# Taking the seven products of a gate-and-up block apart around the plain quarters, with two of its weight sums made by adding DMAs in place

## The chip, the cores and the metric

The kernel runs on one core of one Trainium2 chip. The metric is the device time of one execution in microseconds, lower is better.

## The reference

One layer of a streaming encoder on 256 tokens of width 2048, all in float32:

```python
x = x + 0.5 * swiglu(rms_norm(x, ffn1_norm), ffn1_w_gate, ffn1_w_up, ffn1_w_down)
...  # mixer: S5 state-space heads and stick-breaking attention heads, then w_out
x = x + 0.5 * swiglu(rms_norm(x, ffn2_norm), ffn2_w_gate, ffn2_w_up, ffn2_w_down)
...  # per-layer embedding
def swiglu(h, w_gate, w_up, w_down):
    return (jax.nn.silu(h @ w_gate) * (h @ w_up)) @ w_down
```

The hidden width of each FFN is 5632. The change lies in `h @ w_gate` and `h @ w_up` of both FFNs.

## The kernel before, in words

**Precision by splitting.** Each float32 operand is split into two parts, `hi` and `lo`, and a product is three matmuls: hi x hi, lo x hi, hi x lo. For a weight tile of 128x1024 (two rows of tiles of 512 columns) ScalarE casts `hi` (L181) and VectorE subtracts to get `lo` (L184); this pair of instructions is called a split below. The parts go to a ring of seven pairs of buffers, four named `whi`/`wlo` and three `shi`/`slo` (`weight_pair`), so splits can run ahead of the matmuls.

**Blocks.** `ffn` walks over 11 blocks of 512 hidden columns (`f`). A block multiplies the 256 tokens by a 2048x512 piece of the gate weights and one of the up weights. The depth of 2048 is cut into four quarters of 512 rows; one quarter of one weight is one load of 1 MB into a tile called `raw`, of which there are five. Loads are issued by SP.

**Plain quarters.** `column(side, kbs)` loads quarters `kbs` of gate (side 0) or up (side 1) and multiplies them directly: two halves, each one split and 12 matmuls.

**Groups of seven.** `chunk(kb)` takes quarter `kb` of gate and of up together as a 2x2 block matrix (b11 and b21 are the two halves of the gate quarter, b12 and b22 those of the up quarter) and uses a Strassen-Winograd form: seven products of six matmuls each in place of eight. The products are numbered 1 to 7 by the PSUM bank that they add up in. Four of them need sums of weights:

- product 5: t1 = b11 + b12
- product 6: t2 = t1 + b22
- product 4: t4 = t2 + b21
- product 7: b12 + b22

Before, the first three are made by VectorE in tiles called `sum` (L513), and the fourth by a DMA issued from POOL that adds b22 to b12 in place (L574). The products are traced in the order 1, 5, 6, 4, 2, 3, 7. The matching sums of the activations are made once per FFN (`sum_forms`).

**An ordinary block** is `chunk(0)`, gate quarters 2 and 3 plain, `chunk(1)`, up quarters 2 and 3 plain. Blocks `f` = 6 to 10 of the first FFN and 1 to 10 of the second are ordinary. In the first FFN, blocks 3 and 5 use one group (`single`), and the other early blocks none; in the second FFN block 0 has an order of its own with one `chunk`. The down projections use `chunk` too.

**The end of a block.** `opened` copies bank 1 and makes the running sums with banks 6 and 7, `gated` adds banks 2 and 4, applies Silu and takes bank 5, `ended` adds the double bank 3/8 (L683) and multiplies (L685), and `turned` transposes the result (L217). PSUM has four single banks (`acc`: 1, 2, 4, 5) and two double ones (`aux`: 6/7 and 3/8), all in use in a block.

**Order.** The framework plans the order of each engine's instructions and gives out buffer slots when the program is built; the trace order of the code is the priority. `step()` advances work that was put off (`put_off`) by one step; `tc.issue_after` holds an instruction behind another on its engine.

Of the kernel before, what the change touches and what calls it, by code (L numbers as in the profile page):

```python
# [13 lines left out]
ALU = mybir.AluOpType  # L14
# [19 lines left out]
def layer_kernel(ctx: ExitStack, tc: tile.TileContext, a: dict, shapes: dict, out: bass.AP):  # L34
    nc = tc.nc
# [34 lines left out]
    def com(tag):  # L70
        return get(comp, tag, *{"sg": (1024, 1), "h": (1024, 2), "sq": (NB, 1), "mid": (2048, 1)}[tag])

    def phase(name):
        return tc.tile_pool(name=name, bufs=1, reuse_waits="tile")
# [20 lines left out]
    def start(g):  # L95
        beside.append(g)
        return g

    def step():
        for g in list(beside):  # L100
            if next(g, beside) is beside:
                beside.remove(g)

    def finish(g):
        for _ in g:
            pass

    def put_off(steps, fn, *args):


        def g():
            for _ in range(steps):
                yield
            fn(*args)

        return start(g())
# [169 lines left out]
    ring = [None, 0]  # L286
# [25 lines left out]
    def weight_halves(w, k0, nk, n0, own=None):  # L312

        raw = wp.tile([P, 4, NB], F32, tag="raw", name=uid("raw"), bufs=5)
        nc.sync.dma_start(raw[:, :nk, :], quarter(w, k0 // 4, n0))
        return weight_split(raw, nk, own)

    def gemm_half(ps, half, ts, start, stop, cols=slice(0, NB)):

        (ahi, alo), (h, hi, lo) = half  # L320
        for j in range(2):
            for t in ts:
                lh = ahi[:, 2 * h + j, t * P : (t + 1) * P]
                ll = alo[:, 2 * h + j, t * P : (t + 1) * P]
                nc.tensor.matmul(ps[t], lhsT=lh, rhs=hi[:, j, cols], start=start and j == 0, stop=False)  # L325
                nc.tensor.matmul(ps[t], lhsT=ll, rhs=hi[:, j, cols], start=False, stop=False)  # L326
        for j in range(2):
            for t in ts:
                lh = ahi[:, 2 * h + j, t * P : (t + 1) * P]
                nc.tensor.matmul(ps[t], lhsT=lh, rhs=lo[:, j, cols], start=False, stop=stop and j == 1)  # L330
# [137 lines left out]
    class Seven:  # L468
# [97 lines left out]
        def chunk(self, kb, final=()):  # L566
# [21 lines left out]
                self.product(7, summed(2), b12, final)  # L588
            step()

        def column(self, side, kbs, final=False):

            zs = ((2, 4), (3, 8))[side]
            w, n0 = self.ws[side]
            for kb in kbs:
                part = self.act(kb)
                for half in list(weight_halves(w, 4 * kb, 4, n0)):
                    end = final and kb == kbs[-1] and half[0] == 1
                    for t in range(TT):
                        ps = self.bank(zs[t])  # L600
                        gemm_half({t: ps}, (part, half), (t,), self.begin(zs[t]), end)
                    step()

    shared = (1, 5, 6, 7)

    def ffn(i, xn, nxt, bg=None):
# [4 lines left out]
        alone = (3, 5) if bg else ()  # L611
# [21 lines left out]
        for f in range(NF):  # L633
            for kb, (at, steps) in enumerate(((2, 8), (5, 11))):
                if bg and f == at:
                    put_off(steps, lambda kb: sums.append(sum_forms(sevens, whole_rows(sevens, xn(kb), pinned=True), "h")), kb)
            if prep and f == early:
                finish(prep)
                side.close()
                prep = None  # L640
                turns = pools.enter_context(phase(f"turns{i}"))
                hp = pools.enter_context(phase(f"h{i}b"))
            if f >= early or f in alone:
                sg, hh = com("sg"), com("h")
                gate_cols, up_cols = ([u[:, t * NB : (t + 1) * NB] for t in range(TT)] for u in (sg, hh))

                def opened(s, g=gate_cols, u=up_cols):
                    nc.scalar.copy(g[0], s.bank(1))
                    nc.vector.tensor_tensor(out=u[0], in0=s.bank(6), in1=g[0], op=ALU.add)
                    nc.vector.tensor_tensor(out=u[1], in0=s.bank(7), in1=u[0], op=ALU.add)  # L650

                def gated(s, g=gate_cols, u=up_cols, hh=hh):
                    for z, (ps, other) in enumerate(((s.bank(2), g[0]), (s.bank(4), u[1]))):
                        nc.vector.tensor_tensor(out=g[z], in0=ps, in1=other, op=ALU.add)
                        nc.scalar.activation(g[z], g[z], AF.Silu, scale=xn.rs(z))
                    v = hh.rearrange("p (t n) -> p t n", t=TT)
                    nc.vector.tensor_tensor(
                        out=v, in0=s.bank(5).unsqueeze(1).to_broadcast([P, TT, NB]), in1=v, op=ALU.subtract
                    )

                s = Seven(xn, lambda kb: sums[kb], ((wg, f * NB), (wu, f * NB)), sevens, turns)
                if f == 0:
                    sums.append(sum_forms(sevens, whole_rows(sevens, xn(0))))
                    s.column(0, (1,))
                    s.column(1, (1,))
                    s.chunk(0, shared)
                    put_off(0, opened, s)
                    s.column(0, (2,))
                    s.column(1, (2,))
                    s.column(0, (3,), True)  # L670
                    sums.append(sum_forms(sevens, whole_rows(sevens, xn(1))))
                elif f in alone:
                    s.single(0, gate_cols[0], *up_cols)
                    s.column(0, (1, 2, 3), True)
                else:
                    s.chunk(0)
                    s.column(0, (2, 3))
                    s.chunk(1, (*shared, 2, 4))
                    put_off(0, opened, s)
                put_off(0, gated, s)  # L680

                def ended(s, g=gate_cols, u=up_cols, hh=hh, f=f, hp=hp):
                    nc.vector.tensor_tensor(out=hh, in0=s.banks[3.8], in1=hh, op=ALU.add)  # L683
                    for t in range(TT):
                        nc.vector.scalar_tensor_tensor(  # L685
                            out=u[t], in0=u[t], scalar=xn.rs(t), in1=g[t], op0=ALU.mult, op1=ALU.mult
                        )
                    put_off(2, turned, hp, f, hh)

                s.column(1, (1, 2, 3) if f in alone else (2, 3) if f else (3,), True)  # L690
                if f in alone:
                    put_off(0, ended, s)
                else:
                    ended(s)
                continue


            def gate():
                for t in range(TT):
                    nc.scalar.activation(sg[:, t * NB : (t + 1) * NB], pg[t], AF.Silu, scale=xn.rs(t))  # L700

            first = ()
            if f == 0:
                warm_up(10)
                first = first_quarters(wg, xn)
            pg = gemm_block(xn, wg, f * NB, KD, first)
            sg = com("sg")
            if f == 0:
                for n in range(ND):
                    put_off(n, load_x, n)  # L710
                    put_off(n + 2, xn.squares, n)
                put_off(6, gate)
            else:
                gate()
            pu = gemm_block(xn, wu, f * NB, KD)
            if prep and f == 0:
                start(prep)
            hh = com("h")
            for t in range(TT):
                nc.vector.scalar_tensor_tensor(  # L720
                    out=hh[:, t * NB : (t + 1) * NB], in0=pu[t], scalar=xn.rs(t),
                    in1=sg[:, t * NB : (t + 1) * NB], op0=ALU.mult, op1=ALU.mult,
                )
            put_off(2, turned, hp, f, hh)
# [42 lines left out]
        def summed(kb):  # L767
            if kb not in forms:
                forms[kb] = sum_forms(sevens, rows(kb))
            return forms.pop(kb) if kb == 0 or n else forms[kb]  # L770

        for n in range(0, ND, 2):
# [7 lines left out]
            s = Seven(kept, summed, ((wd, n * NB), (wd, (n + 1) * NB)), sevens, turns)  # L780
            plan = plans[n // 2]
            left = sum(kind == "s" for kind, _ in plan)
            for kind, kb in plan:
                final = (kind, kb) == plan[-1]
# [747 lines left out]
    for n, side in ((0, 0), (1, 0), (0, 1), (1, 1), (2, 0), (2, 1), (3, 0), (3, 1)):  # L1532
        y, r = ((yss, rss), (ysb, rsb))[side]
        ps = next(both) if n < 2 and not side else gemm_block(lambda k: y[k], sides[side], n * NB, SW // P)
        for t in range(TT):
            nc.vector.scalar_tensor_tensor(
                out=xt[t][n], in0=ps[t], scalar=r[0][:, t : t + 1], in1=xt[t][n], op0=ALU.mult, op1=ALU.add
# [73 lines left out]
    with sums_phase("sums3") as sevens:  # L1611
        forms = {1: sum_forms(sevens, whole_rows(sevens, npl(1)), "h")}
        s = Seven(npl, forms.get, ((wg, 0), (wg, NB)), sevens, sevens)
# [29 lines left out]
    s = small(1)  # L1643
# [21 lines left out]
    for c, (ahead, total) in enumerate(((early, part), (part, ms))):  # L1665
# [3 lines left out]
            out=com("sq")[:, :W], in0=gate[:, cols[c]], scalar=1.0, in1=gate[:, cols[c]], op0=ALU.mult, op1=ALU.mult,  # L1669
# [129 lines left out]
```

## Time and profile before

| | |
|---|---|
| median of 3 runs | 1819.23 us (1818.15 to 1820.26) |
| profiled execution | 1818.46 us |
| its span, first to last instruction | 1816.4 us |
| TensorE (PE) busy | 1806.7 us, 99% |
| VectorE (DVE) busy | 1573.9 us, 87% |
| ScalarE (ACT) busy | 1065.3 us, 59% |
| GpSimd (POOL) busy | 106.2 us, 6% |
| granted TensorE clock | 0.999 |

In rows of the profile an instruction is named by its line, engine, operation, and the tiles `out<-in`; `PEld` is the weight load of TensorE, which overlaps the matmuls. A row of instructions by group ends with the busy time, the mean of one in ns, and the idle time of the engine before them. Rows of a timeline begin with the start and the duration in us. A busy time of VectorE is the union of its instructions; the durations of two that follow each other overlap a little. "DMA to landing" is the time from the issue of a DMA to its completion.

The ordinary blocks of the first FFN lie at some 270 to 480 us of the span, those of the second at some 1070 to 1480 us.

### The profile page before, as it was taken

What the parts mean: (1) busy time and instruction counts of PE and PEld (TensorE: products, weight loads), DVE (VectorE), ACT (ScalarE), POOL (GpSimd) and SP (SyncE); (2) the same over time, 40 slices, a digit from 0 to 9 for tenths busy, and PEclk for the clock granted to TensorE, in tenths of its full rate; (3) what the DMA queues carried; (4) which work ended last, traced back from release to release, by engine and by line L of the source; (5) the groups of instructions that cost most, each with busy time, mean ns of one, the idle gap of its engine ahead of it and who ended that gap; (6) DMA issues with size and microseconds to landing.
All of it is one profiled execution on the core that took longest, in us unless ns stands there. A gap on an engine that the chain in (4) does not pass through costs nothing.

```text
span 1816.4 us, 24219 instructions
## 1 busy us (share of the span) xinstructions
PE 1806.7 (99%) x8918; PEld 1496.6 (82%) x8918; DVE 1573.9 (87%) x1839; ACT 1065.3 (59%) x1240; POOL 106.2 (6%) x162
## 2 busy tenths in 40 slices
PE   9999999999999999999999999999999999999998
PEld 7888888888888888888898888888888888888887
DVE  8978889999998896697567899999999999889775
ACT  7445455656565665455695566555565566567664
POOL 0020100000000001110021000000000010000000
PEclk9999999999999999999999999999999999999999
DMA  8799867777776667674636787787767787666563
GB/s 321 268 292 301 269 221 232 235 259 228 262 261 226 190 226 262 188 255 163 218 139 215 234 297 225 263 268 235 232 231 236 241 277 242 220 209 228 195 243 128
DMA packets 107655, 428.41 MB, mean 236 GB/s; under 512 B 24368, under 2 KB 48336, under 8 KB 65136
## 3 DMA queue, kind: packets, MB, share of 16 engines
q1 hardware_dynamic: 96256, 390.06, 60.8%
q0 software_dynamic: 10560, 35.40, 9.0%
q8 instruction: 70, 1.15, 0.2%
q10 hardware_dynamic: 720, 1.41, 0.2%
q14 instruction: 49, 0.40, 0.1%
HBM read 372.41 MB, written 10.88 MB: 211 GB/s over the span
## 4 chain that ended last, share of the span: by engine, by line
PE 96%; DVE 1%; DMA 1%; issue 1%; ACT 1%; SPq 0%; DVEq 0%; ACTq 0%
PE acc L325 16%; PE acc L326 16%; PE acc L330 16%; PE aux L330 7%; PE aux L326 7%; PE aux L325 7%; PE acc L509 5%; PE acc L506 5%; PE acc L507 5%; PE aux L509 3%; PE aux L506 3%; PE aux L507 3%; DMA raw<-in_ffn_w_gate 0%; PE aux L1210 0%; PE acc L1466 0%
## 5 line engine op out<-in xcount | busy, mean ns | idle before, releaser
L184 DVE TENSOR_TENSOR wlo<-raw,whi 128x1024 fp32r<-128x1024 f32 x480 | 580.7, 1222 | 123.5 <-ACT whi L181 120.5
L181 ACT CAST whi<-raw 128x1024 fp32r<-128x1024 f32 x480 | 498.2, 1050 | 291.9 <-PE acc L326 181.8
L325 PE MATMUL acc<-whi,nhi 128*128 128x512 f32 x908 | 356.3, 392 | 2.8 <-ACT whi L277 2.3
L326 PE MATMUL acc<-whi,nlo 128*128 128x512 f32 x908 | 353.7, 390 | 0.0
L330 PE MATMUL acc<-wlo,nhi 128*128 128x512 f32 x908 | 252.5, 389 | 0.0
L184 DVE TENSOR_TENSOR slo<-raw,shi 128x1024 fp32r<-128x1024 f32 x186 | 226.1, 1216 | 15.8 <-ACT shi L181 15.5
L181 ACT CAST shi<-raw 128x1024 fp32r<-128x1024 f32 x186 | 195.2, 1049 | 62.1 <-DMA raw<-in_ffn_w_down 20.3
L325 PEld LDWEIGHTS acc<-whi,nhi 128*128 128x128 f32 x908 | 170.4, 188 | 40.3 <-ACT whi L277 3.5
L330 PEld LDWEIGHTS acc<-wlo,nhi 128*128 128x128 f32 x908 | 170.3, 188 | 35.9 <-DVE wlo L184 0.3
L326 PEld LDWEIGHTS acc<-whi,nlo 128*128 128x128 f32 x908 | 170.5, 188 | 34.8 <-DVE nlo L278 0.3
L181 ACT CAST whi<-sum 128x1024 fp32r<-128x1024 f32 x79 | 83.3, 1054 | 159.6 <-DVE sum L513 141.5
L181 ACT CAST shi<-sum 128x1024 fp32r<-128x1024 f32 x59 | 62.1, 1053 | 104.0 <-DVE sum L513 90.8
L513 DVE TENSOR_TENSOR sum<-sum,raw 128x1024 f32<-128x1024 f32 x92 | 112.1, 1219 | 1.0
L184 DVE TENSOR_TENSOR wlo<-sum,whi 128x1024 fp32r<-128x1024 f32 x79 | 96.2, 1220 | 7.3 <-ACT whi L181 6.7
L574 POOL DMA_DIRECT2D raw<-raw x44 | 38.2, 867 | 1035.7 <-DVE sum L513 595.0
L325 PE MATMUL aux<-whi,nhi 128*128 128x512 f32 x220 | 85.6, 389 | 0.0
L326 PE MATMUL aux<-whi,nlo 128*128 128x512 f32 x220 | 85.6, 389 | 0.0
L184 DVE TENSOR_TENSOR slo<-sum,shi 128x1024 fp32r<-128x1024 f32 x59 | 72.0, 1220 | 1.2 <-ACT shi L181 0.5
L330 PE MATMUL aux<-wlo,nhi 128*128 128x512 f32 x220 | 67.7, 389 | 0.0
L325 PE MATMUL acc<-whi,hhi 128*128 128x512 f32 x156 | 60.7, 389 | 0.0
L326 PE MATMUL acc<-whi,hlo 128*128 128x512 f32 x156 | 60.7, 389 | 0.0
L513 DVE TENSOR_TENSOR sum<-raw,raw 128x1024 f32<-128x1024 f32 x46 | 56.0, 1217 | 5.1 <-DMA raw<-in_ffn_w_down 4.2
(390 smaller groups left out, 3404.1 us busy)
## 6 DMA issues: line engine op xcount, KB each, us to landing
raw<-in_ffn_w_up SPq DMA_DIRECT2D x88, 1024.0 KB, 5.8
raw<-in_ffn_w_down SPq DMA_DIRECT2D x88, 1024.0 KB, 4.9
raw<-in_ffn_w_gate SPq DMA_DIRECT2D x86, 1024.0 KB, 6.9
raw<-in_w_in SPq DMA_DIRECT2D x32, 1024.0 KB, 5.5
raw<-raw POOLq DMA_DIRECT2D x46, 512.0 KB, 5.6
raw<-in_w_out SPq DMA_DIRECT2D x16, 1024.0 KB, 4.9
raw<-in_w_ple_gate SPq DMA_DIRECT2D x16, 1024.0 KB, 5.5
hT<-mid SPq DMA_DIRECT2D x160, 64.0 KB, 4.8
```

The lines of the kernel that those rows point to most:

```text
L181: copy = nc.scalar.copy(hi, src)
L184: rest = nc.vector.tensor_tensor(out=lo, in0=src, in1=hi.bitcast(F32), op=ALU.subtract)
L325: nc.tensor.matmul(ps[t], lhsT=lh, rhs=hi[:, j, cols], start=start and j == 0, stop=False)
L326: nc.tensor.matmul(ps[t], lhsT=ll, rhs=hi[:, j, cols], start=False, stop=False)
L330: nc.tensor.matmul(ps[t], lhsT=lh, rhs=lo[:, j, cols], start=False, stop=stop and j == 1)
L506: nc.tensor.matmul(ps, lhsT=lh[j], rhs=hi[:, j], start=begin and j == 0, stop=False)
L507: nc.tensor.matmul(ps, lhsT=ll[j], rhs=hi[:, j], start=False, stop=False)
L509: nc.tensor.matmul(ps, lhsT=lh[j], rhs=lo[:, j], start=False, stop=z in final and j == 1)
L513: nc.vector.tensor_tensor(out=t, in0=x, in1=y, op=ALU.add)
L574: nc.gpsimd.dma_start(b12, b22, accum_op=ALU.add)
```

## The change

`front`, `middle` and `back` take the place of `chunk` in ordinary blocks; `chunk` stays for the other uses. The order of an ordinary block becomes: products 1, 2, 3 of group 0, gate quarter 2, products 5, 6, 4, gate quarter 3, product 7; then products 1, 2, 3 of group 1, up quarter 2, products 5, 6, 4, 7, up quarter 3. t1 is now made in place in b11 by a second adding DMA from POOL, issued ahead of the one for product 7; t2 and t4 are made by VectorE in place, in b11 and b21. The `sum` tiles are no longer used in these blocks. `opened` and `gated` come one plain quarter before the end of the block, not two.

```diff
+        def front(self, kb, final=()):
+
+            if ring[0] is None:
+                ring[:] = [self.turns, 0]
+            b11, b21, b12, b22 = self.load(kb)
+            whole, summed = self.lefts(kb)
+            self.product(1, whole(0, 0), b11, final)
+            nc.gpsimd.dma_start(b11, b12, accum_op=ALU.add)
+            nc.gpsimd.dma_start(b12, b22, accum_op=ALU.add)
+            step()
+            self.product(2, whole(1, 0), b21, final)
+            self.product(3, summed(3), b22, final)
+            step()
+            return (b11, b21, b12, b22), whole, summed, final
+
+        def middle(self, begun):
+
+            (b11, b21, b12, b22), whole, summed, final = begun
+            self.product(5, summed(0), b11, final)
+            nc.vector.tensor_tensor(out=b11, in0=b11, in1=b22, op=ALU.add)
+            self.product(6, summed(1), b11, final)
+            step()
+            nc.vector.tensor_tensor(out=b21, in0=b11, in1=b21, op=ALU.add)
+            self.product(4, whole(1, 1), b21, final)
+            step()
+
+        def back(self, begun):
+
+            (b11, b21, b12, b22), whole, summed, final = begun
+            self.product(7, summed(2), b12, final)
+            step()
...
-                    s.chunk(0)
-                    s.column(0, (2, 3))
-                    s.chunk(1, (*shared, 2, 4))
+                    begun = s.front(0)
+                    s.column(0, (2,))
+                    s.middle(begun)
+                    s.column(0, (3,))
+                    s.back(begun)
+                    begun = s.front(1, (*shared, 2, 4))
+                    s.column(1, (2,))
+                    s.middle(begun)
+                    s.back(begun)
                     put_off(0, opened, s)
                 put_off(0, gated, s)
...
-                s.column(1, (1, 2, 3) if f in alone else (2, 3) if f else (3,), True)
+                s.column(1, (1, 2, 3) if f in alone else (3,), True)
```

## The prediction

> **What bounds the kernel now.** I read the head of the page first, then busy time by stretches, then the waits of the matmul queue in the two stages that the change touches.
>
> ```profile
> span 1816.4 us, 24219 instructions
> PE 1806.7 (99%) x8918; PEld 1496.6 (82%) x8918; DVE 1573.9 (87%) x1839; ACT 1065.3 (59%) x1240; POOL 106.2 (6%) x162
> PEclk9999999999999999999999999999999999999999
> ```
> ```profile
> 150.00:1700.00 1550.00, 1549.17 (x7756) 1285.68 (x7751) 1361.35 (x1432) 916.53 (x1041) 90.61 (x126) 1.00 0.70 234
> ...
> 1170.14:1251.74 81.60, 81.60 (x362) 67.57 (x360) 78.97 (x77) 47.72 (x51) 3.47 (x4) 1.00 0.74 242
> 1251.74:1333.34 81.60, 81.60 (x362) 67.57 (x360) 79.12 (x77) 48.14 (x51) 3.49 (x4) 1.00 0.76 248
> 1333.34:1414.94 81.60, 81.60 (x362) 67.57 (x360) 78.78 (x77) 46.34 (x50) 3.48 (x4) 1.00 0.74 242
> sum 244.80, PE 244.80 PEld 202.70 DVE 236.87 ACT 142.21 POOL 10.43; mean PE 81.60 PEld 67.57 DVE 78.96 ACT 47.40 POOL 3.48
> ```
> ```profile
> PE acc L509 <- DVE slo L184: 0.4, 1, 0.4
> ```
>
> In the second fence the columns are the stretch, its length, then busy time of PE, weight loads, DVE, ACT and POOL, the granted clock, the DMA share and GB/s. From 150 to 1700 us the matmul queue is idle for 1550.00 - 1549.17 = 0.83 us in all, at a full clock. The three lower stretches are each two gate-and-up blocks of the second FFN: 40.80 us a block, no idle matmul time. A block has 14 products of six matmuls and four plain quarters of 24, so 180 matmuls, and 40.80 / 180 = 0.2267 us each. The last fence is the only wait of the matmul queue between 1040 and 1500 us. So TensorE sets the time, and the edit leaves its 180 matmuls a block as they are. The whole gain within reach is under 0.83 us. What I have to find out is whether the new order still feeds TensorE in time.
>
> By the Trainium skill, page "Trainium Kernel Development and Optimization", section Performance Expectations, busy matmul time is a bad measure of nearness to the limit, and the share of the weight loads a good one. By that rule the 82% of the weight loads would leave room for a gain; but every block here has the same 40.80 us for the same 180 matmuls, and the edit shortens none, so the rule earns only the small chance for "faster" below.
>
> The next engine is VectorE (DVE): 236.87 / 6 = 39.5 us of each 40.8, so 1.3 us are free per block.
>
> **What a block costs on VectorE.** Its instructions in the first of those stretches (two blocks), and their pace when nothing stands between them:
>
> ```profile
> L184 DVE TENSOR_TENSOR wlo<-raw,whi 128x1024 fp32r<-128x1024 f32 x18 | 21.5, 1215 | 0.1
> ...
> L513 DVE TENSOR_TENSOR sum<-sum,raw 128x1024 f32<-128x1024 f32 x8 | 9.7, 1217 | 0.0
> ...
> L513 DVE TENSOR_TENSOR sum<-raw,raw 128x1024 f32<-128x1024 f32 x4 | 4.9, 1216 | 0.0
> L685 DVE SCALAR_TENSOR_TENSOR h<-h,sm,sg 128x512 f32<-128x512 f32 x4 | 2.8, 743 | 0.0
> L217 DVE STREAM_TRANSPOSE mid<-h 128x512 f32<-128x512 f32 x4 | 2.6, 684 | 0.0
> L683 DVE TENSOR_TENSOR h<-aux,h 128x1024 f32<-128x1024 f32 x2 | 2.4, 1220 | 0.1
> ```
> ```profile
> 1161.98 1.22 DVE L184 TENSOR_TENSOR wlo<-raw,whi 128x1024 fp32r<-128x1024 f32 x1
> 1163.12 1.22 DVE L184 TENSOR_TENSOR slo<-raw,shi 128x1024 fp32r<-128x1024 f32 x1
> 1164.26 1.21 DVE L184 TENSOR_TENSOR wlo<-raw,whi 128x1024 fp32r<-128x1024 f32 x1
> ```
>
> A subtraction or a sum of 128x1024 lasts 1.22 us but follows the one before at 1.14 us, so I cost each at 1.14. Each block has 12 / 2 = 6 sums.
>
> **Part 1: one sum of three leaves VectorE in each group.** The edit touches the ordinary blocks: 5 of the first FFN (f = 6 to 10) and 10 of the second (f = 1 to 10), 15 blocks, 30 groups. Two sums a block go: 2 x 1.14 = 2.3 us. The two that stay write in place; their shape is that of the L513 rows, so I cost them as those. VectorE then needs 39.5 - 2.3 = 37.2 us, and 3.6 us of 40.8 are free. By itself this is worth nothing to the time, since no matmul waits for a sum now.
>
> **Part 2: one adding DMA more in each group, in series.** Now b11 += b12 must land before product 5 can be split, and b12 += b22 cannot start before that, since it overwrites what the first reads. The rows are those of the one adding DMA that a group has now, in the second FFN's blocks (1160 to 1480 us), then in the first's (280 to 440 us):
>
> ```profile
> L574 POOL DMA_DIRECT2D raw<-raw x15: 857/867/882, 1167.2 to 1451.7; - x15
> ...
> DMA to landing us min/median/max: 4.5/6.6/7.6
> ...
> L574 POOL DMA_DIRECT2D raw<-raw x8: 847/856/881, 287.6 to 426.9; - x8
> ...
> DMA to landing us min/median/max: 4.5/7.1/9.0
> ```
> ```profile
> q0 software_dynamic: 10560, 35.40, 9.0%
> ```
> ```profile
> raw<-in_ffn_w_up SPq DMA_DIRECT2D x88, 1024.0 KB, 5.8
> ...
> raw<-in_ffn_w_gate SPq DMA_DIRECT2D x86, 1024.0 KB, 6.9
> ```
> ```profile
> L181 ACT CAST whi<-raw 128x1024 fp32r<-128x1024 f32 x480 | 498.2, 1050 | 291.9 <-PE acc L326 181.8 <-PE aux L326 37.0 <-DMA raw<-in_ffn_w_down 17.5
> ```
>
> Call L the time from issue to landing: 6.6 us in ten blocks, 7.1 in five. I take these medians, not the ends 4.5 and 9.0, since they are of the same transfer in the same place; the ends go into the range. POOL's 0.87 us of issue lies inside L, and POOL has 94% of its time free. In the queue behind the second DMA, which waits on POOL for the first, stands only the next group's first.
>
> What the transfers add to the load: 9.0% of 1816.4 us for 35.40 MB is 4.6 us of all 16 engines per MB, 2.4 us for 0.524 MB; two more a block are 4.8 of 40.8 us, so the DMA share goes from about 0.75 to 0.87. It does not fill up, but it speaks for L as now or longer, not shorter.
>
> Now the wait. After product 1's split, VectorE has four splits before product 5's: products 2 and 3 and the two halves of the plain quarter, 4 x 1.14 = 4.6 us. Product 5's cast (1.05 us) starts when the DMA lands, L after product 1's split. So VectorE stands idle for L + 1.05 - 4.6. In the first group of a block the tail of the block before fills this: the aux sum, two multiplications and two transposes, (2.4 + 2.8 + 2.6) / 2 = 3.9 us. In the second group nothing does: opened and gated need products 6 and 7, which come later. Idle time there: 3.1 us at L = 6.6, 3.6 us at 7.1.
>
> Then the second DMA. After the landing VectorE has product 5's split, two sums and the splits of 6 and 4: 1.05 + 5 x 1.14 = 6.75 us. Product 7's split needs the second landing, L after the first, plus the cast: a further idle L + 1.05 - 6.75. In the first group a plain quarter's two splits (2.3 us) lie between and fill it; in the second group product 7 follows product 4 at once. Idle time: 0.9 us at 6.6, 1.4 us at 7.1.
>
> Together VectorE needs 37.2 + 4.0 = 41.2 us a block in the second FFN and 37.2 + 5.0 = 42.2 in the first, against 40.8 of TensorE: late by 0.4 and 1.4 us. **Sum of part 2:** 10 x 0.4 + 5 x 1.4 = 11 us. It comes to nothing where 2L + 2.1 - 4.6 - 6.75 stays under the free 3.6, so for L up to 6.4 us, and the order may let splits of the last quarter go ahead. At the largest landing of the second FFN, 7.6 us, it is 2.4 us in each of 15 blocks, 36 us; at 9.0 us it is 5.2 us, 78 us.
>
> By the Trainium skill, page "DMA: Bandwidth & Descriptors", section "Anatomy of one DMA — SWDGE (gpsimd) path", such a transfer takes about 2.0 us and its bytes at 436 GB/s, which would be 3.2 us for 0.524 MB, and the sum would be 0. The rows disagree: no landing is under 4.5 us.
>
> **Part 3: what is moved.** Products 2 and 3 with their casts and subtractions come ahead of 5, 6 and 4, and the quarters go between. SP issues its eight weight loads a block in the same order as now. But an up tile is held until product 7, a whole quarter longer, and there are five tiles. If the load for the up column's first new quarter has to take that tile, it is issued at product 7's split, while TensorE has products 7, 1, 2 and 3 before it, 4 x 1.36 = 5.4 us; it needs 5.8 + 1.05 us, so the splits must be 1.4 us ahead. How far ahead they are now, at worst (VectorE's subtraction, then the matmul that reads it):
>
> ```profile
> 1241.35 1.18 DVE L184 TENSOR_TENSOR wlo<-raw,whi 128x1024 fp32r<-128x1024 f32 x1
> ```
> ```profile
> 1243.12 0.39 PE L509 MATMUL aux<-wlo,nhi 128*128 128x512 f32 x1
> ...
> 1234.06 0.39 PE L506 MATMUL acc<-shi,hhi 128*128 128x512 f32 x1
> ```
> ```profile
> 1234.26 1.23 DVE L683 TENSOR_TENSOR h<-aux,h 128x1024 f32<-128x1024 f32 x1
> ```
>
> That is 1243.12 - 1242.53 = 0.6 us, at the seventh product of a dense group. In the new order two quarter splits (2.3 us) stand before product 7 against 5.4 us of matmuls, so 3.1 us are gained just there, and I cost the loads at nothing. With that cover gone and a load of 6.9 us, the lack is 2.5 us a block, 38 us.
>
> Product 3 opens the double bank as third product now, 2.7 us into a block, not sixth. The bank is free when the aux sum (begun 0.20 us into the block, 1.23 us long) is done at 1.4 us. One 1.14 us instruction ahead of it fits; a second would make it 1.0 us late, 15 us over 15 blocks. If the other double bank is taken, freed a quarter earlier, nothing. I take nothing.
>
> **The sum.** Span 1816.4, and 2.1 us around it in the profiled execution (1818.46), plus 11 gives 1829.5; the median of the three runs, 1819.23, is 0.8 above that execution: 1830.3 us.
>
> **The rivals.**
> - No change (0.38): the landings stay hidden, because they come under 6.4 us (4.5 is seen) or the last quarter's splits fill the gap. For it: TensorE now runs through blocks in which VectorE has only 1.3 us free, and gets 2.3 more. Against: medians 6.6 and 7.1, and more DMA load. Time 1819.2. This is the side other than my forecast's; it decides at L = 6.4. The 3.2 us of the Trainium skill's page on DMA would lead here too.
> - The tile ring (0.13): the up quarter's load waits for product 7's split and lands late, 38 us: 1857. For it: loads of 5.8 to 6.9 us against 5.4 us. Against: 3.1 us gained just before.
> - The double bank (0.06): 15 us, 1834.
> - Faster (0.03): at most the 0.83 us, so it needs something that no row shows.
>
> **How the numbers follow.** The forecast, VectorE starved by the two landings in a row, has 0.40 and its own range from 1820 to 1855 (L of 6.4 to 7.6). A change under 0.2% (3.6 us) cannot be told from none here. Slower: 0.40 + 0.13 + 0.06 = 0.59; within: 0.38; faster: 0.03. The range goes from the unchanged time, 1817.5, to 1860, past the tile ring; beyond lie the 78 us of 9.0 us landings and the faster case, under 2 in 10 together.
>
> **What would show it.** Of part 1: two sums fewer a block, VectorE busy for 37.2 us of it. Of part 2: 30 more adding DMAs; the casts of products 5 and 7 waiting for raw<-raw, most in the second group; the matmul queue waiting for casts and subtractions by some 0.4 to 1.4 us a block, which makes blocks of 41.2 to 42.2 us. Landings under 6.4 us, or blocks of 40.8 us, prove the forecast wrong. Waits of the matmul queue behind loads of in_ffn_w_up would show the tile ring; behind L683, the double bank.

## The result, and the profile after

The changed kernel takes 1944.47 us (1944.03 to 1946.56, four runs), the kernel before 1819.10 in the same rounds: a ratio of 1.0691, 95% interval 1.0673 to 1.0710. The change costs 125 us, where 11 were forecast. The head of the page, and busy time by stretches with the columns as in the prediction:

```profile
span 1942.3 us, 24188 instructions
PE 1856.1 (96%) x8918; PEld 1508.9 (78%) x8918; DVE 1543.1 (79%) x1809; ACT 1061.5 (55%) x1240; POOL 131.8 (7%) x192
PEclk9999999999999999999999999999898999999999
```
```profile
150.00:1700.00 1550.00, 1471.58 (x7232) 1192.22 (x7215) 1220.36 (x1288) 836.50 (x952) 113.61 (x153) 0.98 0.71 226
265.00:560.00 295.00, 270.38 (x1128) 214.66 (x1127) 233.52 (x226) 147.79 (x156) 22.40 (x29) 0.97 0.76 231
560.00:1090.00 530.00, 529.92 (x3056) 443.13 (x3055) 411.01 (x478) 327.41 (x410) 39.35 (x53) 1.00 0.63 214
1090.00:1620.00 530.00, 476.28 (x1954) 373.75 (x1953) 406.20 (x400) 255.29 (x272) 38.95 (x48) 0.96 0.74 226
```

The span grew by 1942.3 - 1816.4 = 125.9 us. PE idle grew from 9.7 to 86.2 us, by 76.5. The other 49.4 us stand in the same 8918 matmuls: PE is busy for 1856.1 in place of 1806.7. The granted clock tells of much of it: 1.00 in the stretch between the two FFNs, 0.97 and 0.96 where the ordinary blocks are. In the trace's clock records the clock is at half in 12 stretches of 3.41 or 6.83 us, 61.4 us in all, and PE is busy for 53.7 us of them at half the pace, so about 27 us are lost to it; before there is none in these stages. Where the other 22 us of longer busy time come from was not followed up. VectorE, which the forecast made the bound, is less busy than before.

What the matmul queue waits for, and below it what the casts and subtractions wait for (in total us, times, longest):

```profile
PE acc L506 <- ACT shi L181: 18.7, 8, 4.5
PE acc L506 <- ACT whi L181: 18.6, 8, 4.0
PE aux L506 <- ACT whi L181: 14.8, 9, 3.0
PE aux L506 <- ACT shi L181: 6.2, 7, 1.3
PE acc L325 <- DVE sg L686: 5.7, 2, 3.3
PE acc L506 <- DVE sg L686: 5.4, 6, 1.4
```
```profile
DVE wlo L184 <- ACT whi L181: 232.1, 128, 8.1
...
ACT whi L181 <- DMA raw<-raw: 127.4, 22, 9.0
...
ACT shi L181 <- DMA raw<-raw: 67.7, 16, 8.0
...
ACT whi L181 <- DVE raw L610: 33.9, 12, 5.0
```

The chain is read from below: the casts wait for the adding DMAs (`raw<-raw`) and for the in-place sum that makes product 6's weights (L610), VectorE waits for the casts, and so does the first matmul of a product (L506). The row of the first adding DMA (L598, b11 += b12), by its source line:

```profile
L598 POOL DMA_DIRECT2D raw<-raw x30: 852/858/882, 266.6 to 1574.7; - x30
...
who waited for it (us, times):
  POOL raw L599: 148.8, 17
  ACT whi L181: 93.5, 16
  ACT shi L181: 54.0, 11
...
DMA to landing us min/median/max: 4.6/9.4/11.5
```

Its median is 9.4 us, longer than any landing quoted before the change; the second (L599) has 4.5/5.5/12.2. Adding up, in the 14 ordinary blocks whose order of products could be followed in the trace, what each matmul started later than 0.2267 us after the one before it gives 113 us: in group 0 39.4 at product 4, 15.4 at product 6, 11.3 in the plain quarter behind product 4, 6.8 at product 2; in group 1 23.6 at product 4, 12.5 at product 6, 2.8 at product 7. Product 5, for which the first DMA works, costs nearly nothing: the plain quarter ahead of it still feeds PE.

**One block in detail.** SP's loads and POOL's adding DMAs, then ScalarE, VectorE and PE (start, duration, and in brackets the idle time before with its releaser), in group 0 of a block of the second FFN:

```profile
1340.20 1.46 SPq L315 DMA_DIRECT2D raw<-in_ffn_w_gate  x2
1343.61 0.33 SPq L520 DMA_DIRECT2D raw<-in_ffn_w_gate  x1
```
```profile
1345.12 0.86 POOL L598 DMA_DIRECT2D raw<-raw  x1 [11.04 <-DVE wlo L184]
1356.06 0.89 POOL L599 DMA_DIRECT2D raw<-raw  x1 [10.08 <-DMA raw<-raw]
```
```profile
1355.76 1.05 ACT L181 CAST whi<-raw 128x1024 fp32r<-128x1024 f32 x1 [8.72 <-DMA raw<-raw]
```
```profile
1356.85 1.23 DVE L184 TENSOR_TENSOR wlo<-raw,whi 128x1024 fp32r<-128x1024 f32 x1 [5.20 <-ACT whi L181]
1357.99 1.22 DVE L689 TENSOR_TENSOR h<-acc,h 128x1024 f32<-128x1024 f32 x1
1359.12 1.22 DVE L610 TENSOR_TENSOR raw<-raw,raw 128x1024 f32<-128x1024 f32 x1
1360.26 1.22 DVE L721 TENSOR_TENSOR h<-aux,h 128x1024 f32<-128x1024 f32 x1
1361.53 1.22 DVE L184 TENSOR_TENSOR slo<-raw,shi 128x1024 fp32r<-128x1024 f32 x1
1362.67 1.41 DVE L723 SCALAR_TENSOR_TENSOR h<-h,sm,sg 128x512 f32<-128x512 f32 x2
1364.00 1.30 DVE L217 STREAM_TRANSPOSE mid<-h 128x512 f32<-128x512 f32 x2
1365.22 1.18 DVE L613 TENSOR_TENSOR raw<-raw 128x1024 f32<-128x1024 f32 x1
```
```profile
1367.53 0.80 PE L506 MATMUL acc<-whi,hhi 128*128 128x512 f32 x1 [3.99 <-ACT whi L181]
```

The DMA is issued at 1345.12, when product 1's subtraction has read b11; three loads of 1 MB were issued in the 5 us before. It lands after 10.6 us. Then everything is a chain: product 5's cast and subtraction, the in-place sum for product 6, its split, the in-place sum for product 4 (L613). Between them stand pieces of the end of the block before (L689, L721, L723, L217). VectorE is busy without a gap from 1356.85 on, and still product 4 comes 4 us late. By stretches just behind that:

```profile
1360.00:1367.40 7.40, 2.94 (x11) 1.48 (x9) 7.35 (x9) 2.96 (x4) 0.00 (x0) 0.87 0.07 15
1367.40:1370.80 3.40, 3.27 (x8) 2.60 (x9) 3.40 (x4) 3.40 (x5) 0.00 (x0) 0.50 0.60 120
...
1374.20:1377.60 3.40, 3.40 (x17) 2.82 (x16) 1.67 (x3) 2.00 (x2) 0.00 (x0) 1.00 1.10 218
```

After the gap the clock is 0.50 for a whole stretch: 8 matmuls in 3.4 us where the row with the full clock has 17. The Trainium skill, page "TensorE: Matmul & The Clock Gate", section "Part 1: The HAM clock gate", has the clock at half after an idle window of about 3.4 us and until some 3.4 us of work. The trace agrees on half and on steps of 3.41 us; single gaps of 2.24 to 3.00 us brought it too, so one gap need not be 3.4 us long.

In group 1 the order on the engines adds to it. POOL, then the casts, then VectorE:

```profile
1278.55 0.87 POOL L599 DMA_DIRECT2D raw<-raw  x1 [5.79 <-issue]
```
```profile
1290.42 1.04 ACT L181 CAST whi<-raw 128x1024 fp32r<-128x1024 f32 x1 [7.69 <-DMA raw<-raw]
```
```profile
1281.62 1.23 DVE L613 TENSOR_TENSOR raw<-raw 128x1024 f32<-128x1024 f32 x1
1282.76 1.23 DVE L184 TENSOR_TENSOR wlo<-raw,whi 128x1024 fp32r<-128x1024 f32 x1
1291.49 1.23 DVE L184 TENSOR_TENSOR wlo<-raw,whi 128x1024 fp32r<-128x1024 f32 x1 [7.51 <-ACT whi L181]
```

Product 4's sum (L613) is ready at 1282.85, but its cast does not follow: in the order that the planner made, product 7's split stands ahead of product 4's. Its cast waits for the second landing and starts at 1290.42, 11.9 us after that DMA's issue and 7.6 us after product 4's sum was ready.

### The profile page after: what moved, and what is told of

Its sections match the earlier page's. It is cut to its first block, busy times and chain, and to the rows that moved or that the text cites. A ratio compares the mean times of both kernels' runs of the same rounds, so it can differ in the third digit from the quotient of the medians.

```text
span 1942.3 us, 24188 instructions
## 1 busy us (share of the span) xinstructions
PE 1856.1 (96%) x8918; PEld 1508.9 (78%) x8918; DVE 1543.1 (79%) x1809; ACT 1061.5 (55%) x1240; POOL 131.8 (7%) x192
## 3 DMA queue, kind: packets, MB, share of 16 engines
q0 software_dynamic: 14880, 51.13, 12.5%
## 5 line engine op out<-in xcount | busy, mean ns | idle before, releaser
L184 DVE TENSOR_TENSOR wlo<-raw,whi 128x1024 fp32r<-128x1024 f32 x531 | 642.3, 1225 | 231.8 <-ACT whi L181 229.0
L181 ACT CAST whi<-raw 128x1024 fp32r<-128x1024 f32 x531 | 549.0, 1049 | 504.3 <-PE acc L326 177.6
L181 ACT CAST shi<-raw 128x1024 fp32r<-128x1024 f32 x225 | 233.6, 1048 | 187.4 <-DMA raw<-raw 67.7
L184 DVE TENSOR_TENSOR slo<-raw,shi 128x1024 fp32r<-128x1024 f32 x225 | 273.2, 1220 | 74.1 <-ACT shi L181 68.5
L330 PEld LDWEIGHTS acc<-wlo,nhi 128*128 128x128 f32 x912 | 172.1, 189 | 36.2
L506 PE MATMUL acc<-whi,hhi 128*128 128x512 f32 x140 | 56.7, 405 | 14.0 <-ACT whi L181 10.3
L325 PE MATMUL acc<-whi,hhi 128*128 128x512 f32 x156 | 60.8, 390 | 2.4 <-DVE sg L686 2.4
L326 PE MATMUL acc<-whi,hlo 128*128 128x512 f32 x156 | 60.7, 389 | 0.0
L325 PE MATMUL aux<-whi,hhi 128*128 128x512 f32 x152 | 59.1, 389 | 0.0
L326 PE MATMUL aux<-whi,hlo 128*128 128x512 f32 x152 | 59.1, 389 | 0.0
L184 DVE TENSOR_TENSOR hlo<-hT,hhi 128x1024 fp32r<-128x1024 f32 x44 | 53.7, 1221 | 3.9 <-ACT hhi L181 3.9
L598 POOL DMA_DIRECT2D raw<-raw x30 | 25.9, 862 | 449.1 <-DVE wlo L184 242.1
L506 PE MATMUL acc<-shi,hhi 128*128 128x512 f32 x92 | 38.3, 416 | 18.4 <-ACT shi L181 17.5
L507 PE MATMUL acc<-whi,hlo 128*128 128x512 f32 x140 | 55.7, 398 | 0.0
```

Source lines behind the costliest of these rows:

```text
L181: copy = nc.scalar.copy(hi, src)
L184: rest = nc.vector.tensor_tensor(out=lo, in0=src, in1=hi.bitcast(F32), op=ALU.subtract)
L506: nc.tensor.matmul(ps, lhsT=lh[j], rhs=hi[:, j], start=begin and j == 0, stop=False)
L507: nc.tensor.matmul(ps, lhsT=ll[j], rhs=hi[:, j], start=False, stop=False)
L598: nc.gpsimd.dma_start(b11, b12, accum_op=ALU.add)
```

## The experiments

All are timed against the kernel before in common rounds. The texts on record use letters: A is the late landing of the first adding DMA, the others stand for the theory that the same text describes.

**The order alone.** The new order of the products and quarters, with the sums as before (three by VectorE in tiles of their own, one adding DMA):

```diff
-            nc.gpsimd.dma_start(b11, b12, accum_op=ALU.add)
+            t1 = self.add(b11, b12)
             nc.gpsimd.dma_start(b12, b22, accum_op=ALU.add)
...
-            nc.vector.tensor_tensor(out=b11, in0=b11, in1=b22, op=ALU.add)
+            t2 = self.add(b11, b22)
...
-            nc.vector.tensor_tensor(out=b21, in0=b11, in1=b21, op=ALU.add)
+            t4 = self.add(t2, b21)
```


> The new order alone: products 1, 2, 3, plain quarter, 5, 6, 4 and so on, but the sums as before (three by VectorE in sum tiles, one adding DMA for product 7). Theory A (the first adding DMA lands too late, behind weight loads that were issued at the same moment, and products 6 and 4 wait for the sums made from it): no such DMA is left, so 1817 to 1826 us. Rival B (the order itself costs: up tiles held longer, PSUM banks freed later, the block's tail in front of the sums): still above 1890 us. Rival C (two landings in a row starve VectorE before product 7, the prediction's term): 1817 to 1826 us, like A.

1818.86 us, ratio 1.0004 (0.9994 to 1.0013). The order costs nothing and earns nothing; the double bank and the tile ring of the prediction's rivals are no matter of the order.

**Each adding DMA by itself.** First the first one replaced by a sum in place on VectorE, then the second:

```diff
-            nc.gpsimd.dma_start(b11, b12, accum_op=ALU.add)
+            nc.vector.tensor_tensor(out=b11, in0=b11, in1=b12, op=ALU.add)
             nc.gpsimd.dma_start(b12, b22, accum_op=ALU.add)
```


> The changed kernel with only its first adding DMA (b11 += b12) replaced by a sum of VectorE in place; order, in-place sums and the second adding DMA stay, VectorE makes three sums as before. Theory A (the first landing comes too late for products 6 and 4): 1817 to 1826 us, no wait of the matmul queue at products 6 and 4. Rival D (writing the sums in place is itself a cost, since the raw tiles are then held until product 4): above 1840 us.

1831.43 us, ratio 1.0066 (1.0051 to 1.0081). Of the 125 us, 113 go with the first adding DMA. It is 12.6 us above the run of the order alone, which differs from it only in that t1, t2 and t4 have tiles of their own: that is what the sums in place cost, more than A had said and less than D. In place, a sum must wait until the split of the product before has read the tile; the casts wait 86.2 us, in 25 waits, for the sum of product 6 (L610). They also wait longer for loads of `in_ffn_w_up` (41.6 us against 14.9 with the order alone). Which of the two makes the 12.6 us was not separated.

```diff
-            nc.gpsimd.dma_start(b12, b22, accum_op=ALU.add)
...
+            nc.vector.tensor_tensor(out=b12, in0=b12, in1=b22, op=ALU.add)
             self.product(7, summed(2), b12, final)
```


> The changed kernel with its second adding DMA replaced by a sum of VectorE in place just before product 7; the first stays. A: the first DMA still lands late, perhaps a little sooner with less traffic, so most of the loss stays, 1890 to 1945 us. B: no change, 1935 to 1950. C: the second landing was the cause, so 1820 to 1840 us.

1915.02 us, ratio 1.0528 (1.0513 to 1.0544): the second DMA carries 29 us beside the first. Without the first it costs nothing that shows, since the run of the order alone has it too; so the 113 and the 29 us do not add up. The first lands as late as in the changed kernel, by its source line:

```profile
DMA to landing us min/median/max: 4.5/9.4/11.8
```

**Fewer loads beside it.** The plain quarters read one kept tile:

```diff
+                        keep[0] = wp.tile([P, 4, NB], F32, tag="raw", name=uid("raw"), bufs=5)
+                        nc.sync.dma_start(keep[0], quarter(wg, 2, f * NB))
...
-                    s.column(0, (2,))
+                    s.column(0, (2,), kept=keep[0])
```


> The changed kernel with the plain quarters of ordinary blocks multiplied from one weight tile that is loaded once per FFN, so four of eight weight loads a block are left out (four raw tiles are left for the rest) and the result is another. A: with fewer loads queued beside it the first adding DMA lands in 4.5 to 6.5 us instead of 9.4, and the time falls to 1820 to 1850 us. B: the order is the same, so it stays above 1900. C: both landings get shorter, 1820 to 1850.

1866.16 us, ratio 1.0263 (1.0247 to 1.0278). The row of the first adding DMA:

```profile
DMA to landing us min/median/max: 4.5/5.9/9.2
```

The adding DMAs and sums are the same, and 78 of 125 us are gone: most of the loss hangs on the loads beside the DMA, and the landing's median falls with them. They change something else too: the casts wait 4.7 us for loads of `in_ffn_w_up`, 36.2 in the changed kernel. How much of the 78 us that makes was not separated. But 47 us stay, so with a median of 5.9 us, under the 6.4 us at which the prediction had put the loss at nothing, the kernel is still well behind.

**The same DMA, earlier.** One adding DMA, b12 += b11, issued about a plain quarter and a product earlier, when the group's tiles have been loaded and before product 1; product 7's sum goes to a tile of its own:

```diff
+        def ready(self, kb):
...
+            b11, b21, b12, b22 = self.load(kb)
+            seven = self.add(b12, b22)
+            nc.gpsimd.dma_start(b12, b11, accum_op=ALU.add)
...
                     s.middle(begun)
+                    s.ready(1)
                     s.column(0, (3,))
```


> One adding DMA per group as in the second run (b12 += b11 here, for product 5), but the tiles are loaded and this DMA is issued about one plain quarter and a product ahead of the group, since it no longer waits for product 1's split; VectorE makes product 7's sum into a sum tile and the other two in place, so three sums. A: the landing is as late after its issue as ever, 6 to 10 us, but in time for products 6 and 4, so 1817 to 1835 us, against 1915 with the same count of DMAs and sums issued after product 1. If the adding DMA as such is the cost (contention with the weight loads, rival G): 1890 us or more.

1840.98 us, ratio 1.0117 (1.0102 to 1.0132), against 1915.02 with the same numbers of adding DMAs and sums: 74 us are back, so an adding DMA is not dear in itself. Not all of the 74 belong to the earlier issue: this run also takes product 7's sum out from behind the landing, and holding that sum back earns 32 us alone in a run below. A's range is missed by 6 us. The landing is 5.5 us in the median, up to 11.0; of the 22 us above the kernel before, PE's waits explain about 16 (21.1 us in all their rows, against 4.8 before), the largest of them for casts; which sum makes those late was not settled.

**More matmuls ahead of the sums.** In group 0 both gate quarters come before products 5, 6 and 4:

```diff
-                    s.column(0, (2,))
+                    s.column(0, (2, 3))
                     s.middle(begun)
-                    s.column(0, (3,))
                     s.back(begun)
```


> The changed kernel with both gate quarters of group 0 ahead of products 5, 6 and 4, so that the first DMA of group 0 has two plain quarters (10.9 us of matmuls) of cover instead of one; group 1 is untouched. A: the waits at products 6 and 4 of group 0 go (with the slow matmuls behind them some 66 of the 113 us counted in 14 blocks), 1865 to 1885 us. B: tiles are held still longer and the loads come later, 1945 us or more. C: product 7 now follows product 4 at once in both groups, so the second landing shows twice, 1950 to 1980 us.

1889.54 us, ratio 1.0391 (1.0374 to 1.0408): 55 us better than the change, and above A's range by 5 us. Products 6 and 4 of group 0, late by 54.8 us in the changed kernel, are late by under 2 us here, as A had it; group 1 still has 24.7 us at product 4, and its product 7 becomes later (11.3 us). Waits for the bank (`PE acc L506 <- DVE sg L686`) grew from 5.4 to 9.4 us.

**Product 7 held behind product 4, and the tail put off.**

```diff
+            copied, rest = self.last
+            with tc.issue_after(copied), tc.issue_after(rest):
-            self.product(7, summed(2), b12, final)
+                self.product(7, summed(2), b12, final)
```


> The changed kernel with product 7's cast and subtraction held behind product 4's on their engines (in group 1 the planned order has them ahead of product 4's, so product 4 stands behind the wait for the second landing). If that order carries the second landing's part of the loss (E, order of product 7 and 4): group 1's waits go, 36 of 113 us counted there, so 1905 to 1920 us, the same as the run in which VectorE made that sum. If it is the landing as such (C), holding product 7 back only moves the wait to product 7: 1935 us or more.

1931.77 us, ratio 1.0615 (1.0597 to 1.0633): 13 us better, between both expectations. Product 4 of group 1 falls from 23.6 to 0.9 us of late matmuls, so the reading of the order was right; but product 2 of the next block is later instead (from 6.8 to 17.6 us), and product 7 (from 2.8 to 5.2).

```diff
-                    for t in range(TT):
-                        nc.vector.scalar_tensor_tensor(
...
-                    put_off(2, turned, hp, f, hh)
+                    def rest():
+                        for t in range(TT):
+                            nc.vector.scalar_tensor_tensor(
...
+                        put_off(0, turned, hp, f, hh)
...
+                        put_off(5, rest)
```


> The one before, and the multiplications and transposes of a block's tail put off by five steps, so that on VectorE they no longer stand between product 5's subtraction and the sum for product 4 in group 0 (2.6 us there). If the tail's place matters (F): 1.5 to 2.6 us a block less than the run before, 20 to 40 us, so 1870 to 1895. If the landing alone sets the end of group 0 (A): within 8 us of the run before.

1917.91 us, ratio 1.0544 (1.0526 to 1.0562), 14 us better still and again in between: product 4 of group 0 falls from 37.6 to 15.2 us, while the plain quarter after product 3 (18.7, nearly all of it in two blocks) and product 7 of group 1 (15.5) become late.

**The tail by itself.** To read it without the second DMA, the late tail (the second edit above) was put into the kernel with one adding DMA (b11 += b12, the sum for product 7 on VectorE).

> Edit: the kernel with only the first adding DMA left (the second sum on VectorE, 1915.0 us) with the tail of the block before (the products of gate and up and its transposes) put off by five steps. Theory F, the tail stands on VectorE between product 5's subtraction and the sums of products 6 and 4, so that the late landing and the tail add up: of the 56 us that products 6 and 4 and the matmuls after them at half clock lost in group 0, 25 to 45 go, 1870 to 1890 us. Theory A alone, only the landing (median 9.4 us, which stays) counts, and the tail runs where VectorE would wait anyway: at most 10 us less, 1905 us or more.

1925.68 us, ratio 1.0584 (1.0568 to 1.0600): 11 us worse than without it (1915.02). That is within A's bound, but for a reason that neither theory had. Its timeline of VectorE and the row of the matmul queue that grew:

```profile
1281.38 0.68 DVE L681 TENSOR_TENSOR h<-aux,sg 128x512 f32<-128x512 f32 x1
1288.90 1.22 DVE L619 TENSOR_TENSOR raw<-raw 128x1024 f32<-128x1024 f32 x1 [6.83 <-DMA raw<-raw]
1290.04 0.68 DVE L682 TENSOR_TENSOR h<-aux,h 128x512 f32<-128x512 f32 x1
1290.64 0.68 DVE L686 TENSOR_TENSOR sg<-acc,sg 128x512 f32<-128x512 f32 x1
```
```profile
PE acc L506 <- DVE sg L686: 38.9, 12, 7.0
```

With the tail moved, the planner put product 7's sum (L619) ahead of the sums that free the banks. It waits for the landing, and L686 behind it; the matmul queue waits up to 7.0 us for the bank. So the sum was held behind product 4's subtraction, with the late tail and, as control, without:

```diff
+            copied, rest = self.last
+            with tc.issue_after(rest):
-            nc.vector.tensor_tensor(out=b12, in0=b12, in1=b22, op=ALU.add)
+                nc.vector.tensor_tensor(out=b12, in0=b12, in1=b22, op=ALU.add)
             self.product(7, summed(2), b12, final)
```


> Edit: as the run with one adding DMA and the late tail (1925.7 us), and product 7's sum on VectorE is held behind product 4's subtraction. There it stood on VectorE ahead of the sums that free the banks and waited for the landing (83.7 us in 19 waits), so the tail's share could not be read. Theory F (the tail between product 5's subtraction and the sums costs group 0 its time): 20 to 40 us below the control, 1870 to 1895 us. Theory A (only the landing counts, the tail runs where VectorE waits anyway): within 10 us of the control.

> Control for the run before: one adding DMA, product 7's sum held behind product 4's subtraction, the tail where the changed kernel has it. Both theories: the sum had waited only 10.7 us for the landing in the kernel without the hold (1915.0 us), so 1900 to 1920 us.

With the late tail 1872.72 us, ratio 1.0296 (1.0280 to 1.0313); the control 1883.07 us, ratio 1.0352 (1.0329 to 1.0376). The control's expectation was missed by 17 us: holding one sum earns 32 us over 1915.02. Part of that may be the landing, 8.3 us in the median in place of 9.4; how much was not separated. The late tail nets 10 us, not 20 to 40, and its landing is shorter as well (7.3 us in the median), so not even the 10 us are the tail's place alone. The net hides two opposite parts. Products 6 and 4 of group 0 and the plain quarter behind them fall from 39.0 to 14.8 us of late matmuls, by 24 us, as theory F had it. But the plain quarter behind product 3 is late by 15.5 us in their place, all of it in two of the 15 blocks. In these two the planned order of ScalarE has product 5's cast ahead of the quarter's casts, and it waits for the landing:

```profile
1185.38 1.04 ACT L181 CAST shi<-raw 128x1024 fp32r<-128x1024 f32 x1 [9.24 <-DMA raw<-raw]
```

So the tail in front of the sums costs products 6 and 4 of group 0 some 24 us here, and by the same count 36 us (60.4 to 24.2) in the two runs before; the order on the engines takes more than half of that back. It is a part of the loss, and not the greater one.

**All three at once.** Fewer loads, product 7 held and the tail put off, the edits as above:

> Edit: the changed kernel with the three suspected causes taken away together: four of eight loads of a block left out (the plain quarters read one kept tile, so the output differs), product 7's split held behind product 4's, and the tail put off by five steps. If these three account for the loss: the 47 us that fewer loads left above the kernel before lay at product 4 of both groups (23 us) and at product 2 of group 0 (11 us), so that 20 to 30 us go, 1836 to 1846 us. If each only hands its wait on to the next product, as holding and putting off did beside all loads (they won 27 of an expected 45 us or more): 1850 us or more, with product 2 and product 7 late in place of product 4.

1843.72 us, ratio 1.0140 (1.0123 to 1.0156): within the first range. The landing and the longest waits of the matmul queue:

```profile
DMA to landing us min/median/max: 4.5/5.9/8.1
```
```profile
PE acc L506 <- DVE sg L689: 7.2, 4, 2.3
PE acc L325 <- DVE sg L689: 6.4, 2, 3.5
```

No cast delays a product by more than 1.2 us now; what is left of the waits is for banks 2 and 4, which `gated` frees (L689, 13.6 us). So 101 of the 125 us hang on these three, by far the most on the loads, and the other 25 us stay.

## Why the prediction was wrong, by its own steps

- **What bounds the kernel** held: the order alone gives 1818.86 us, and no run was faster than the kernel before.
- **Part 1** held: VectorE has 30 instructions and 30.8 us less, and no run shows a gain from it.
- **Part 2, the value of L, is the step that failed first.** I took 6.6 and 7.1 us because the rows were "of the same transfer in the same place". It is the same transfer, but not in the same place: the old DMA is issued when VectorE's sum for product 5 has read its tile, the new one when product 1's subtraction has read it, in 21 of 30 cases close behind two or three weight loads. It lands in 9.4 us in the median, beyond the 9.0 us that had been the longest landing considered (78 us, outside the range). The doubt was named ("speaks for L as now or longer") and given no price of its own.
- **The same part, "the tail of the block before fills this".** Group 0 has not the covered but the dearest gap. The tail does run there, but in front of the sums too; moving it took 24 us from products 6 and 4 and the quarter behind them, and netted 10.
- **The same part, the model.** I compared sums of VectorE's work in a block with PE's 40.8 us. By it, with 9.4 and 5.5 us for the two landings, group 1 has 9.4 + 1.05 - 4.6 = 5.9 us of idle and none before product 7; 37.2 + 5.9 is 2.3 us over 40.8, 34 us in 15 blocks, not 125. So the size of L explains 23 of the 114 us by which the forecast was short; the larger failure is the form of the sum. The rest is what a balance over a block can't hold: the casts and in-place sums of products 5, 6 and 4 form one serial chain behind the landing, and PE runs dry within it while VectorE has work on either side. Hence the waits at products 6 and 4, not at 5 and 7, and mostly in group 0.
- **The order on the engines** was taken from the trace order of the code. `chunk` holds product 7's split behind product 3's with `issue_after`; `back` leaves this hold out, and the planner put product 7's split ahead of product 4's. Holding it behind product 4's won 13 us.
- **A gap costs more than its length.** No term stood for the clock; it lost about 27 us.
- **The in-place sums** were priced as sums of the same shape. They cost 12.6 us, in waits of their own or in later loads.
- **The rivals.** "No change" had its point at L = 6.4; the median lies above it, and at 5.9 us 47 us were still lost, so the point itself was wrong. The order, and with it the tile ring, costs nothing. The double bank costs nothing either: the matmul queue of the changed kernel never waits for L721, the sum that frees it (L683 before). The two rows for L686, 11.1 us, are single banks 2 and 4, which `gated` frees; with the order alone they are one row of 1.6 us, so they come with the late sums and not with product 3's new place. Blocks of 41.2 to 42.2 us were to show the forecast; they last 44 to 56 us, from one L721 of the ends of blocks to the next.

## What to carry to other kernels

A transfer's landing time belongs to the moment of its issue: before moving one, look at which loads are released at the new moment, since it may start only when the older of them are through. When a balance per block leaves an engine free time, follow the one longest chain from landing to matmul as well, with all its waits in place, and ask what stands between its links in each engine's order. Gaps of a few us on TensorE should be charged with the time at half clock that follows.

## What the hardware showed that was not expected

**The adding DMA starts only when the older loads ahead of it are through.** From the DMA records of the 30 first adding DMAs, grouped by the loads of 1 MB issued in the 6 us before: with one load (9 of them) the first packet starts 1.44 to 1.69 us after the issue; with two (5) 2.44 to 3.87; with three (16) 4.56 to 5.17, after 1.48 to 1.68 MB of the loads have moved. That is their rate, some 0.33 MB/us. In these 16 the first packet comes within 1.6 us of the landing of the second of the three loads, before or after it, and 2.9 to 5.8 us before the third lands. In all 30 the last load lands only after the adding DMA's first packet. With three loads the two then share the way: 0.22 to 1.64 MB of loads move between the first packet and the landing, which takes 4.4 to 6.8 us, against 3.1 to 6.0 with one load. Of the 44 such DMAs issued at L574 before the change, none had three. In the run with four loads fewer a block, the median fell with the loads. By the Trainium skill, page "DMA: Bandwidth & Descriptors", section "Queues, rings and completion order", a DMA engine takes turns between its queues packet by packet; the adding DMA should then start amid the loads. These records show it amid the youngest load, but not amid the older ones. Whether it is held in the queues or before its descriptors are made, no run here tells.

**The clock.** The changed kernel has 12 stretches at half, in steps of 3.41 us, 61.4 us in all. Each follows a gap of 2.24 to 4.53 us on the matmul queue, but not every gap brings one: none follows those of 2.05, 2.38 and 3.33 us. With the first sum on VectorE no wait of the matmul queue in these stages was over 1.4 us, and the clock stayed full.
